# Attention scores and value products for two heads in turn, in the two halves of the array

## Chip, cores and metric

The kernel runs on one core of a Trainium2 chip. The metric is the device time of one execution in microseconds; lower is better. The core has a matrix engine (TensorE, in the profile PE for products and PEld for the loading of its stationary operand, called weights here), VectorE (DVE), ScalarE (ACT), GpSimd (POOL) and the transfer queues (SP among them). TensorE writes to eight banks of its accumulation memory, called P0 to P7 below.

## What is computed

One transformer layer in float32, for 256 tokens of 1024 features: an adaptive modulation, a token mixer (attention and retention beside each other, gated and projected), a norm, a gated feed-forward part with a short convolution, and another norm. The change concerns the attention alone. With 256 tokens there is one block, so the block selection of the reference falls away and what remains is causal softmax attention of 8 heads of 64 features:

```python
    def chunk(i):
        ...
        l_own = jnp.einsum('bhqd,bhkd->bhqk', qc, k_own).astype(jnp.float32) * scale
        l_own = jnp.where(causal, l_own, NEG_BIG)
        ...
        p = jax.nn.softmax(logits, axis=-1).astype(v.dtype)
        ...
        return (jnp.einsum('bhqk,bhkd->bhqd', p_own, v_own)
        ...
```

Queries and keys are rotated (rotary embedding) before; the outcome goes through `w_proj_moba`.

## The kernel before

**Main stream.** Nearly all time goes into products with weights that are read once. They arrive as units of 2048 columns (1 MB) in four `raw` buffers (`load_raw`, L71), and each unit is split into two halves of 1024 columns. A half is split into a high and a low part: ScalarE writes the high part (`whi`, L1001), VectorE the rest (`wlo`, L1015). `mm3` (L79 to L82) multiplies a tile by three matmuls: high by high, high by low, low by high. There are eight buffers for halves, and a planner (`prep_to`) keeps six halves split ahead of the products. The list `steps` holds one entry a half; the loop at the end of `_body` takes them in order. In attention's stretch a half is 12 matmuls of 512 columns, or 24 of 256. VectorE also reduces slices of `w_ada` (`ada`, L147) between the halves.

**Side streams.** Attention is a generator, `mixers()`, which the loop resumes three times a step: before the splits, after them, and after the products. Instructions are issued in the order of the program, each engine has its own queue in that order, and semaphores hold an instruction until its data are there. One turn `i` of the loop in `mixers()` (L801) is one step of the main stream. In it:

- before the splits, ScalarE scales the rows of head i-2 by one over their sum (L806) and takes exponentials of head i-1 (L810);
- after the splits, VectorE takes the reciprocal of the sums (L814); TensorE transposes the three 128 x 128 blocks of head i-TL (L819, TL = 4), and ScalarE copies them out (L821) to one of two buffers, 9a and 9b in turn;
- TensorE multiplies the values of head i-TL-1 by them (L831 with 256 moving columns, L832 with 128). The output has 64 rows; even heads take partitions 0 to 63 of P6, odd heads 64 to 127. After an odd head, `split` (L65, L66) brings the pair out as high and low parts;
- TensorE computes the scores of head i (L840, twice: 128 queries by 128 keys, and 128 by 256). The operands have 64 rows: partitions 0 to 63 of `qkT` hold an even head, 64 to 127 the odd one. Even heads write to P4, odd ones to P7. VectorE adds the mask and takes the maximum in one instruction for each of the two pieces (L847), and scales the maxima (L850);
- later parts of retention (`rope`, `rot_T` at L757) follow in some steps; then come the products of the step's half.

So scores run at i = 0 to 7, transposes at i = 4 to 11, and values at i = 5 to 12. Operands of attention are f32 and not split; the profile shows each such matmul as two loads of weights and two matmuls of the same line. Matmuls of the main stream are marked `fp32r` at their inputs and show one of each.

In the profile, `128*128`, `64*128` and `128*64` behind a matmul are the rows and columns of the array that it uses.

Of the kernel before, what the change touches and what calls it, by code (L numbers as in the profile page):

```python
# [13 lines left out]
HM, DM = 8, 64  # L14
# [36 lines left out]
def _body(nc, a, out, pe, act, dve, sp, cst, wts, big, tmp, ps, dram):  # L51
# [8 lines left out]
    def halves(n):  # L60
        """A [128, 8, 256] operand as two tiles of four k-tiles."""
        return [slot(n + e, [128, 4, 256], F32R) for e in "ab"]
# [21 lines left out]
    def table(func):  # L84
        """Brings the table of a function in ahead of its use."""
        d_ = tmp.tile([128, 1], F32, name="dummy", bufs=1)
        act.activation(d_, epst, func)

# [36 lines left out]
    # silu(c) along every partition  # L125
# [6 lines left out]
    def rows(dst, cols):  # L132
        """dst[every partition, 128 i + p] = cols[p, i]."""
        for c in range(2):
            p = bank(6 + c)
            for i in range(4):
                pe.transpose(p[:, i * 128:(i + 1) * 128],
                             cols[:, c * 4 + i:c * 4 + i + 1].to_broadcast([128, 128]), ident)
            act.activation(dst[:, c * 512:(c + 1) * 512], p, AF.Copy)
# [4 lines left out]
    def ada(raw, sec, j, rows=slice(0, 1024)):  # L144
        """Feature tile j of section sec of the modulation, its features on partitions."""
        junk = tmp.tile([128, 1024], mybir.dt.bfloat16, name="junk", bufs=1)
        dve.tensor_tensor_reduce(out=junk[:, rows], in0=raw[:, rows], in1=srow[:, rows], scale=1.0, scalar=0.0,  # L147
                                 op0=OP.mult, op1=OP.add, accum_out=mod[:, sec, j:j + 1])

# [6 lines left out]
    def h1(j, part):  # L156
        """Feature tile j of x (1 + scale) + shift."""
        if part == 0:
            ra = raws.pop(("ada1", j))
            if j == 0:  # L160
                ada(ra, 0, 0, slice(0, 512))
                dve.tensor_tensor(bcol[:, 0, 0:1], bcol[:, 0, 0:1], mod[:, 0, 0:1], OP.add)
            for i in range(2):
                ada(ra[:, i * 1024:(i + 1) * 1024], i, j, slice(512 if i == j == 0 else 0, 1024))
            dve.tensor_tensor(mod[:, 0:2, j], mod[:, 0:2, j], bcol[:, 0:2, j], OP.add)
            load_A()
        else:
            h32 = slot(("7a", "7b")[j % 2], [128, 256])
            act.activation(h32, raws.pop(("xT", j)), AF.Identity, scale=mod[:, 0, j:j + 1],
                           bias=mod[:, 1, j:j + 1])  # L170
            split(hh[:, j], hl[:, j], h32)
# [22 lines left out]
    def products_X(u):  # L194
        """The first gate's columns, of two feature tiles, in the banks that q and k leave for them. Two of
        them share a bank, so a product with zeros begins both."""
# [33 lines left out]
    main = []       # units: (source, None) or a slice of w_ada: (source, fn)  # L230
    steps = []      # (halves needed, halves done with, fn of their tiles)

    def weights(src, mm0, mm1):
        """A unit of two halves of 1024 columns; each is split, then used."""
        n = 2 * len(main)
        main.append(src)
        for i, mm in enumerate((mm0, mm1)):
            steps.append(((n + i,), (n + i,), lambda ts, mm=mm: mm(*ts[0])))

    def weights4(srcs, fns, needs):  # L240
        """Units whose halves are each used in several steps."""
# [132 lines left out]
    class Norm:  # L374
        """z = ALPHA x + g y piece by piece, its statistics and (z - mean) / std."""
# [22 lines left out]
        def more(self, c, w, p):  # L398
            """The rest of a sum of which add() had a part."""
# [15 lines left out]
        def shift(self):  # L415
            """-mean / std, for the scalar engine."""
            dve.tensor_scalar(self.sd[:, 2:3], self.mu, self.rstd, -1.0, op0=OP.mult, op1=OP.mult)
            self.nmr = self.sd[:, 2:3]
# [32 lines left out]
    def ln1_T(t):  # L451
        """Transposes of the normed tokens; scale and shift of the second modulation on the way out."""
# [9 lines left out]
    def ln1_hi(t, ks, whole=False):  # L462
        """On the scalar engine, the high parts, or the whole."""
# [14 lines left out]
    def ln1_half(t, c):  # L478
        """Four feature tiles; the two engines read different banks at a time."""
# [18 lines left out]
    def xs_group(src, xh, xl, t_bank, hooks):  # L498
        """Eight k-tiles x 512 columns, all of token tile 0 before token tile 1; with the high parts of a
        token tile before its low parts."""  # L500
# [45 lines left out]
    def out_tok1(q):  # L546
        """A quarter of the columns of token tile 1, so that little is left after the last product."""
# [19 lines left out]
    gh2, gl2 = (lambda k: S["h2h"][k // 4][:, k % 4]), (lambda k: S["h2l"][k // 4][:, k % 4])  # L567

    def up_tokens(t, p):
        """The first four tiles of the up projection come by tokens; turned here."""  # L570
# [61 lines left out]
    def out_rows(n, t, cs):  # L632
        """(z - mean) g / std + b, and the store; the first step of a piece comes before the second of the
        one before it, the first of all beside the square root."""
# [30 lines left out]
    def tok1(c, w):  # L665
        """The last quarter of the columns has a bank of its own for the last rounds, so that little is
        left after the last product."""
# [46 lines left out]
    later = []  # L714

    def ada_unit(secs, u, done):
        """Unit u (two feature tiles) of a section of w_ada; done() comes some steps after the last."""
# [7 lines left out]
    def rows_done(sec):  # L725
        """The section as a row on every partition, by way of DRAM: its features are eight to a partition."""
# [5 lines left out]
    def rope(x, cos, sin, pairs):  # L732
        """x = x * cos + (partner of x) * (signed sin) for heads of cos's length."""
# [19 lines left out]
    def rot_T(roped, t, dst, which, b):  # L753
        """Transposes of half a token tile's roped columns into dst[feature, group, token]."""
# [21 lines left out]
    def mixers():  # L776
        """Attention and retention beside the main stream. A step of the stream resumes this three
        times: before its splits, after them, and after its products."""
# [21 lines left out]
        blk = [slice(128 * qb, 128 + 256 * qb) for qb in range(2)]  # L800
        for i in range(HM + TL + 2):  # L801
# [11 lines left out]
            if 0 <= i - 1 < HM:  # L813
                dve.reciprocal(mx[:, 6:8], mx[:, 4:6])  # L814
            if 0 <= i - TL < HM:
# [7 lines left out]
            if 0 <= i - TL - 1 < HM:  # L823
                h = i - TL - 1
                pT = pt.pop(h)
                if h % 2 == 0:
                    S["pv"] = bank(6)
                p = S["pv"]
                s = slice(64 * (h % 2), 64 * (h % 2) + 64)
                c = slice(64 * h, 64 * h + 64)  # L830
                pe.matmul(p[s, 0:256], v[:, 0, c], pT[:, 0:256], start=True, stop=False)  # L831
                pe.matmul(p[s, 128:256], v[:, 1, c], pT[:, 256:384], start=False, stop=True)  # L832
                if h % 2:
                    split(yah[:, h // 2], yal[:, h // 2], p[:, 0:256])
            if i < HM:
                s = slice(64 * (i % 2), 64 * (i % 2) + 64)
                g = i // 2
                p = bank(4 + 3 * (i % 2))
                for qb, c in enumerate(blk):
                    pe.matmul(p[:, c], qkT[0][s, g, qb * 128:(qb + 1) * 128],  # L840
                              qkT[1][s, g, :128 + 128 * qb], start=True, stop=True)
                if i == 0:
                    sms = S["sms"] = slot(11, [128, TL + 2, 384])
                sm = sms[:, i % (TL + 2)]
                mx = tmp.tile([128, 8], F32, name="mx", bufs=TL + 2)
                for qb, c in enumerate(blk):
                    dve.tensor_tensor_reduce(out=sm[:, c], in0=p[:, c], in1=consts["mask"][:, 128 - 128 * qb:],  # L847
                                             scale=1.0, scalar=-3.0e38, op0=OP.add, op1=OP.max,
                                             accum_out=mx[:, qb:qb + 1])
                dve.tensor_scalar(mx[:, 2:4], mx[:, 0:2], -0.125, None, op0=OP.mult)  # L850
                st[i] = sm, mx
# [92 lines left out]
    def residual():  # L944
        """x1 = norm * g + b, and the rows of the second norm on all partitions."""
# [16 lines left out]
    # where the slices of w_ada for the later parts come in the stream  # L962
# [17 lines left out]
    def prep_halves():  # L980
        """Splits the halves in turn; the first part of one comes before the second of the one before it,
        where there is a buffer for it."""
# [177 lines left out]
```

## Time and profile before

| what | value |
|---|---|
| time, median of 3 runs | 445.71 us (445.6 to 446.73) |
| span of the profiled execution | 444.4 us |
| median less span | 1.3 us |
| TensorE busy | 427.8 us, 2732 matmuls |
| VectorE busy | 346.9 us |
| ScalarE busy | 242.2 us |
| attention's steps with scores or values | about 88 to 142 us |

The span is the time from the first to the last instruction of the execution that the profiler recorded; the time of a run holds some more on both sides. Busy time is the union of an engine's instructions. Matmuls overlap in the records, since one starts while the one before it still drains, so the distance from one start to the next says more than their length. The chain of waits gives that distance: every piece ends where the next one begins.

### The profile page before, as it was taken

How to read it: one execution, taken by the hardware profiler on the slowest of the kernel's cores; microseconds unless marked ns; L12 is line 12 of the kernel's file. 1: busy time of each engine (PE TensorE's matmuls, PEld its weight loads, DVE VectorE, ACT ScalarE, POOL GpSimd, SP SyncE). 2: the span in 40 equal slices, each digit the busy share in tenths (PEclk: the TensorE clock that was granted, in tenths of full speed). 3: DMA queues.
4: the chain of work that ended last, by engine and by line, in shares of the span. 5: the costliest groups of instructions: out<-in, count | busy, mean ns of one | idle time of the engine just before them, and what ended most of it. 6: DMA issues, size and time to landing. Idle time of an engine off the chain costs nothing.

```text
span 444.4 us, 6901 instructions
## 1 busy us (share of the span) xinstructions
PE 427.8 (96%) x2732; PEld 383.2 (86%) x2732; DVE 346.9 (78%) x547; ACT 242.2 (55%) x368; POOL 7.3 (2%) x17
## 2 busy tenths in 40 slices
PE   2999999999999999999999999999999999999993
PEld 1778888877777899999988899999999999999883
DVE  4888789976895989798788888698896765566476
ACT  4376578587774457643443896555454454455500
POOL 0000000000000000000000010000000000000000
PEclk9999999999999999999999999999999999999998
DMA  7999996886347678868745149577657764640001
GB/s 259 406 385 355 329 347 265 318 306 252 128 170 303 237 249 318 328 253 331 287 169 201 46 158 383 219 269 296 254 223 270 292 243 154 227 175 16 1 24 71
DMA packets 19728, 105.72 MB, mean 238 GB/s; under 512 B 2528, under 2 KB 4592, under 8 KB 8432
## 3 DMA queue, kind: packets, MB, share of 16 engines
q1 hardware_dynamic: 18288, 100.27, 60.2%
q0 software_dynamic: 1408, 5.01, 3.3%
q8 instruction: 21, 0.34, 0.3%
q14 instruction: 11, 0.09, 0.1%
HBM read 104.22 MB, written 1.06 MB: 237 GB/s over the span
## 4 chain that ended last, share of the span: by engine, by line
PE 92%; DVE 3%; DMA 2%; ACT 1%; SPq 1%; issue 0%; DVEq 0%
PE P L80 28%; PE P L82 27%; PE P L81 27%; DMA raw<-in_ada 2%; DVE junk L147 2%; PE P L840 2%; PE P L831 1%; PE P L757 1%; PE P L513 1%; PE P L515 1%; PE P L516 1%; SPq L73 1%; PE P L819 1%; DVE wlo L66 1%; ACT whi L65 0%; PE P L890 0%
## 5 line engine op out<-in xcount | busy, mean ns | idle before, releaser
L1015 DVE TENSOR_TENSOR wlo<-raw,whi 128x1024 fp32r<-128x1024 f32 x118 | 140.6, 1221 | 24.7 <-ACT whi L1001 24.7
L1001 ACT ACTIVATE whi<-raw 128x1024 fp32r<-128x1024 f32 x118 | 120.3, 1052 | 38.7 <-PE P L82 11.9
L82 PE MATMUL P<-whi,A 128*128 128x512 f32 (+1 forms) x228 | 87.2, 382 | 0.0
L80 PE MATMUL P<-whi,A 128*128 128x512 f32 (+1 forms) x184 | 73.0, 396 | 5.9 <-ACT A L65 5.7
L81 PE MATMUL P<-wlo,A 128*128 128x512 f32 (+1 forms) x184 | 70.8, 385 | 0.0
L147 DVE CUSTOM_DVE_ANT_0 junk<-raw,srow 128x1024 bf16<-128x1024 f32 (+1 forms) x49 | 58.8, 1200 | 1.5 <-DMA raw<-in_ada 1.1
L80 PE MATMUL P<-A3a,whi 128*128 128x256 f32 x192 | 54.4, 283 | 0.0
L80 PE MATMUL P<-A3b,whi 128*128 128x256 f32 x192 | 54.3, 283 | 0.0
L81 PE MATMUL P<-A6b,whi 128*128 128x256 f32 x192 | 54.3, 283 | 0.0
L82 PE MATMUL P<-A3b,wlo 128*128 128x256 f32 x192 | 54.3, 283 | 0.0
L82 PE MATMUL P<-A3a,wlo 128*128 128x256 f32 x192 | 54.3, 283 | 0.0
L81 PE MATMUL P<-A6a,whi 128*128 128x256 f32 x192 | 54.3, 283 | 0.0
L82 PEld LDWEIGHTS P<-whi,A 128*128 128x128 f32 x228 | 43.3, 190 | 8.8 <-DVE A L66 0.2
L80 PEld LDWEIGHTS P<-whi,A 128*128 128x128 f32 x184 | 35.1, 191 | 16.4 <-ACT A L65 7.6
L80 PE MATMUL P<-A,whi 128*128 128x256 f32 x160 | 45.9, 287 | 0.0
L82 PE MATMUL P<-A,wlo 128*128 128x256 f32 x160 | 45.2, 283 | 0.0
L81 PE MATMUL P<-A,whi 128*128 128x256 f32 x160 | 45.2, 283 | 0.0
L81 PEld LDWEIGHTS P<-wlo,A 128*128 128x128 f32 x184 | 35.1, 191 | 6.1
L81 PEld LDWEIGHTS P<-A6a,whi 128*128 128x128 f32 x192 | 36.8, 192 | 0.3
L80 PEld LDWEIGHTS P<-A3a,whi 128*128 128x128 f32 x192 | 36.8, 192 | 0.3
L80 PEld LDWEIGHTS P<-A3b,whi 128*128 128x128 f32 x192 | 36.9, 192 | 0.0
L81 PEld LDWEIGHTS P<-A6b,whi 128*128 128x128 f32 x192 | 36.9, 192 | 0.0
(231 smaller groups left out, 713.1 us busy)
## 6 DMA issues: line engine op xcount, KB each, us to landing
raw<-in_ada SPq DMA_DIRECT2D x23, 1024.0 KB, 6.2
raw<-in_wup SPq DMA_DIRECT2D x11, 1024.0 KB, 4.8
raw<-in_wgate SPq DMA_DIRECT2D x11, 1024.0 KB, 5.0
raw<-in_wdown SPq DMA_DIRECT2D x11, 1024.0 KB, 4.8
raw<-in_winB SPq DMA_DIRECT2D x10, 1024.0 KB, 5.8
raw<-in_winA SPq DMA_DIRECT2D x16, 256.0 KB, 7.0
raw<-in_winA SPq DMA_DIRECT2D x4, 1024.0 KB, 7.2
raw<-in_winGr SPq DMA_DIRECT2D x4, 1024.0 KB, 5.3
```

The source lines that it names most:

```text
L66: dve.tensor_tensor(lo, src, f(hi), OP.subtract)
L73: sp.dma_start(t[:, i * n:(i + 1) * n], src[:, i * n:(i + 1) * n])
L80: pe.matmul(o, lh, rh, start=start, stop=False)
L81: pe.matmul(o, lh, rl, start=False, stop=False)
L82: pe.matmul(o, ll, rh, start=False, stop=stop)
L147: dve.tensor_tensor_reduce(out=junk[:, rows], in0=raw[:, rows], in1=srow[:, rows], scale=1.0, scalar=0.0, op0=OP.mult, op1=OP.add, accum_o ...
L513: pe.matmul(p, xl(k)[:, tk], hi[:, c], start=False, stop=k == 7)
L515: pe.matmul(p, xh(k)[:, tk], hi[:, c], start=k == 0, stop=False)
L516: pe.matmul(p, xh(k)[:, tk], lo[:, c], start=False, stop=False)
L840: pe.matmul(p[:, c], qkT[0][s, g, qb * 128:(qb + 1) * 128], qkT[1][s, g, :128 + 128 * qb], start=True, stop=True)
L1001: act.activation(hi, src, AF.Copy)
L1015: dve.tensor_tensor(lo, src, f(hi), OP.subtract)
```

## The change

Scores are computed for a pair of heads in the steps with even i, up to 6; values for a pair at i = 6, 8, 10 and 12. Within a pair the matmuls of the two heads take turns: first piece of the even head, first piece of the odd head, second piece of each. The even head uses the lower half of the array's rows (scores) or columns (values), the odd head the upper half. Scores still go to P4 and P7, values to P6. The value products now stand ahead of the transposes of the same step, not behind them. VectorE's masking of both heads follows the scores of the pair. Transposes, exponentials and scaling stay one head a step.

The core of the diff (the rest takes out comments and docstrings):

```diff
+        def scores(h):
+            ps2 = [bank(4), bank(7)]
+            for qb, c in enumerate(blk):
+                for e in range(2):
+                    s = slice(64 * e, 64 * e + 64)
+                    pe.matmul(ps2[e][:, c], qkT[0][s, h // 2, qb * 128:(qb + 1) * 128],
+                              qkT[1][s, h // 2, :128 + 128 * qb], start=True, stop=True)
+            for e in range(2):
+                sm = S["sms"][:, (h + e) % (TL + 2)]
+                mx = tmp.tile([128, 8], F32, name="mx", bufs=TL + 2)
+                for qb, c in enumerate(blk):
+                    dve.tensor_tensor_reduce(out=sm[:, c], in0=ps2[e][:, c],
+                                             in1=consts["mask"][:, 128 - 128 * qb:],
+                                             scale=1.0, scalar=-3.0e38, op0=OP.add, op1=OP.max,
+                                             accum_out=mx[:, qb:qb + 1])
+                dve.tensor_scalar(mx[:, 2:4], mx[:, 0:2], -0.125, None, op0=OP.mult)
+                st[h + e] = sm, mx
+
+        def attend(h):
+            p = bank(6)
+            pT = [pt.pop(h + e) for e in range(2)]
+            for kb, (o, c) in enumerate(((slice(0, 256), slice(0, 256)), (slice(128, 256), slice(256, 384)))):
+                for e in range(2):
+                    pe.matmul(p[64 * e:64 * e + 64, o], v[:, kb, 64 * (h + e):64 * (h + e) + 64], pT[e][:, c],
+                              start=kb == 0, stop=kb == 1)
+            split(yah[:, h // 2], yal[:, h // 2], p[:, 0:256])
+
...
             if 0 <= i - 1 < HM:
                 dve.reciprocal(mx[:, 6:8], mx[:, 4:6])
+            if i % 2 == 0 and 0 <= i - TL - 2 < HM:
+                attend(i - TL - 2)
             if 0 <= i - TL < HM:
...
-            if 0 <= i - TL - 1 < HM:
-                h = i - TL - 1
-                pT = pt.pop(h)
-                if h % 2 == 0:
-                    S["pv"] = bank(6)
-                p = S["pv"]
-                s = slice(64 * (h % 2), 64 * (h % 2) + 64)
-                c = slice(64 * h, 64 * h + 64)
-                pe.matmul(p[s, 0:256], v[:, 0, c], pT[:, 0:256], start=True, stop=False)
-                pe.matmul(p[s, 128:256], v[:, 1, c], pT[:, 256:384], start=False, stop=True)
-                if h % 2:
-                    split(yah[:, h // 2], yal[:, h // 2], p[:, 0:256])
-            if i < HM:
...
+            if i < HM and i % 2 == 0:
                 if i == 0:
...
+                    S["sms"] = slot(11, [128, TL + 2, 384])
+                scores(i)
```

More of the change, by code (lines that the diff above doesn't have):

```diff
@@ L822, in mixers @@
                 pt[i - TL] = pT
-            if 0 <= i - TL - 1 < HM:
-                h = i - TL - 1
-                pT = pt.pop(h)
-                if h % 2 == 0:
-                    S["pv"] = bank(6)
-                p = S["pv"]
-                s = slice(64 * (h % 2), 64 * (h % 2) + 64)
-                c = slice(64 * h, 64 * h + 64)
-                pe.matmul(p[s, 0:256], v[:, 0, c], pT[:, 0:256], start=True, stop=False)
-                pe.matmul(p[s, 128:256], v[:, 1, c], pT[:, 256:384], start=False, stop=True)
-                if h % 2:
-                    split(yah[:, h // 2], yal[:, h // 2], p[:, 0:256])
-            if i < HM:
[L836 to L841, printed above, removed]
-                if i == 0:
[L843 to L851, printed above, removed]
+            if i < HM and i % 2 == 0:
+                if i == 0:
+                    S["sms"] = slot(11, [128, TL + 2, 384])
+                scores(i)
             if 0 <= i - RROPE < 4:
```

## The prediction

> **What bounds the kernel now.** I read the page first (part 1), then busy time by stage, then the waits of TensorE, to see whether TensorE is short of time or of work in the stage of the change.
>
> ```profile
> PE 427.8 (96%) x2732; PEld 383.2 (86%) x2732; DVE 346.9 (78%) x547; ACT 242.2 (55%) x368; POOL 7.3 (2%) x17
> ```
>
> ```profile
> 88.00:92.00 4.00, 4.00 (x18) 2.72 (x17) 2.65 (x8) 3.33 (x6) 0.00 (x0) 1.00 1.02 377
> ...
> 109.00:114.00 5.00, 5.00 (x25) 3.62 (x26) 4.07 (x11) 3.85 (x11) 0.00 (x0) 1.00 0.52 205
> 114.00:119.00 5.00, 5.00 (x25) 3.62 (x25) 4.49 (x12) 3.77 (x10) 0.00 (x0) 1.00 0.53 210
> 119.00:124.00 5.00, 5.00 (x25) 3.58 (x24) 4.25 (x11) 2.89 (x9) 0.00 (x0) 1.00 0.00 0
> 124.00:129.00 5.00, 5.00 (x29) 3.93 (x28) 4.93 (x10) 2.90 (x7) 0.00 (x0) 1.00 0.56 210
> 129.00:134.00 5.00, 5.00 (x29) 3.92 (x28) 4.59 (x9) 4.97 (x9) 0.00 (x0) 1.00 0.62 221
> ...
> 300.00:400.00 100.00, 100.00 (x728) 95.20 (x727) 72.09 (x97) 48.18 (x60) 1.08 (x2) 1.00 0.64 237
> ```
>
> ```profile
> PE P L80 <- ACT A L65: 5.7, 2, 5.4
> PE P L137 <- DVE sc L130: 3.1, 1, 3.1
> ```
>
> The columns of the windows are: length, then PE, weight loader, VectorE, ScalarE, GpSimd, then granted clock, share of DMA, GB/s. In each stage of attention TensorE is busy for the whole window at clock 1.00, and its only data waits, 8.8 us of two kinds, all lie in the first 60 us (asked for 60 us to the end, the view of waits has no row). So TensorE is the bound, and the question is what its busy time holds. The transfers are full at 88 to 92 us (1.02) and empty at 119 to 124 (0.00): by then they are ahead, and wait for buffers.
>
> A busy TensorE is not one that streams. The chain of waits gives each piece the time until the next one, and around the attention matmuls it is uneven:
>
> ```profile
> 81.23 0.88 PE P L757 x8
> ...
> 88.45 0.85 PE P L840 x4
> 89.30 0.43 PE P L80
> 89.73 0.23 PE P L81
> ...
> 107.78 0.33 PE P L819 x3
> 108.11 0.57 PE P L831 x2
> 108.90 0.85 PE P L840 x4
> 109.75 0.43 PE P L80
> 110.18 0.23 PE P L81
> ...
> 112.71 0.33 PE P L819 x3
> ...
> 122.89 0.57 PE P L831 x2
> 123.68 0.43 PE P L80
> ...
> 127.78 1.02 PE P L757 x8
> ...
> 142.00 0.63 PE P L890 x2
> ...
> 146.90 0.43 PE P L890 x2
> ```
>
> ```profile
> 107.39 0.48 PEld L819 LDWEIGHTS P<-first,A 128*128 128x128 f32 x3
> 108.04 0.19 PEld L831 LDWEIGHTS P<-A9a,A 128*64 128x64 f32 x2 [0.17 <-issue]
> 108.31 0.35 PEld L832 LDWEIGHTS P<-A9a,A 128*64 128x64 f32 x2
> 108.83 0.52 PEld L840 LDWEIGHTS P<-A3b,A3a 64*128 64x128 f32 x4 [0.17 <-issue]
> 109.68 0.19 PEld L80 LDWEIGHTS P<-whi,A 128*128 128x128 f32 x1 [0.33 <-issue]
> ```
>
> An f32 matmul appears as two passes (x2 for the one at L831, x4 for the two at L840). With 256 moving columns it takes 0.43 us in a steady run (146.90), with 128 columns 0.22 (L832: 108.90 - 108.11 - 0.57). I call the passes b = 0.215 and a = 0.11. One head's scores, or its values, are two passes of each: 0.65 us. The scores piece takes 0.85, so **0.20 us goes before its first pass**; the main product behind it takes 0.43 where 0.23 is usual, so **0.20 goes on the way out**. The values take 0.57 + 0.22 = 0.79: 0.14 on the way in. Out of them it is 0.20 before a matmul of the whole array (123.68, and 0.63 against 0.43 at L890), 0.14 before transposes (1.02 against 0.88). The loader's rows say why: at each change of the used part of the array (128 x 128, 128 x 64, 64 x 128) it is idle for "issue", though no data is missing, and the next weights are loaded after the array has emptied instead of beside the last pass. All this lies on the path.
>
> **Before, in sum.** Scores 8 x 0.85 = 6.80; out of scores 8 x 0.20 = 1.60; values 8 x 0.79 = 6.32; out of values in the five steps i = 8 to 12 that have no scores behind them 3 x 0.20 + 2 x 0.14 = 0.88. Together 15.60 us of TensorE.
>
> **The change part by part.** *Fewer changes of shape.* No matmul is added or dropped: 16 for scores and 16 for values remain. But scores come in 4 groups for 8 and values in 4 for 8. If a group's passes ran one after the other, as within one head today, a scores group would be 0.20 + 4a + 4b + 0.20 = 0.20 + 1.30 + 0.20 = 1.70, four of them 6.80. A values group is 0.14 + 1.30, four of them 5.76; out of it to the transposes three times 0.14 and once 0.20, 0.62. Together 13.18: **2.4 us saved without any overlap**, by rows of this trace, provided a change between the two halves costs nothing.
>
> *Overlap of the two halves.* No row shows two halves in flight at once, so this is bounded: nothing (13.18), or both heads wholly at once, 0.65 for a pair: 4 x 1.05 + 4 x 0.79 + 0.62 = 7.98, 7.6 us saved. Below nothing is the third rival. I take a value between, by the order of issue. The two passes of one matmul use the same half and stand next to each other, so the order is e0 e0 e1 e1 e0 e0 e1 e1. A pass starts no earlier than the one issued before it and not before its own half is free. For values (b b b b a a a a) the third pass then runs beside the second and the fifth and sixth beside the fourth; the last ends at 3b + 2a = 0.865. Loading does not disturb this: two loads of 64 columns start 0.055 apart (108.04: two of 0.134 in 0.19). For scores (a a a a b b b b) the passes alone would allow 2a + 3b = 0.865, but loads of 128 columns start 0.11 apart (four of 0.19 in 0.52), as long as an a pass. If the loader does one at a time, the first four passes cannot overlap, and only the seventh runs beside the sixth: 4a + 3b = 1.085. I take that, being the nearest row, and 0.865 as its other end (0.9 us over four groups).
>
> Scores 4 x (0.20 + 1.085 + 0.20) = 5.94; values 4 x (0.14 + 0.865) + 0.62 = 4.64; together 10.58. **Saved 15.60 - 10.58 = 5.0 us.** The profiled span is 444.4 us and the median of the runs 445.71, 1.3 us of it around the span; the difference carries over whole: 439.4 and **440.7**.
>
> The Trainium skill ("TensorE: Matmul & The Clock Gate", Part 3: Packing small matmuls) gives a packed group the length of one matmul plus about 4 ns for each further tile. By that the sum would be the upper end, 438.1 us. No row here shows it, and it is stated of neighbours that lie in different tiles, where here every second neighbour lies in the same one.
>
> *Order.* Values now stand ahead of the same step's transposes. They wait for ScalarE's copy of the step before, with that step's transposes, scores and all its main products queued behind on TensorE. The copy is early:
>
> ```profile
> 108.15 0.49 ACT L821 ACTIVATE A9b<-P 128x384 f32<-128x384 f32 x1 [1.12 <-PE P L819]
> ```
>
> It ends at 108.64, while the next step's attention begins with the transposes of 112.71, 4.1 us later; with steps shortened by a microsecond 3 us remain. Cost nothing; without that cover at most the copy's 0.49 in four steps, 2.0 us. The buffers turn over as before: the two score banks are written again two steps later, the transposed pair is read before its buffers are refilled.
>
> *VectorE.* The odd head's masking moves one step ahead:
>
> ```profile
> 104.87 0.29 DVE L847 CUSTOM_DVE_ANT_0 A<-P,mask 128x128 f32<-128x128 f32 x1 [0.94 <-PE P L840]
> ...
> 105.55 0.17 DVE L850 TENSOR_SCALAR mx<-mx 128x2 f32<-128x2 f32 x1
> ```
>
> That is 0.85 us a head, so even steps get 0.85 more and odd steps 0.85 less. From 109 to 134 us VectorE is busy for 22.3 of 25 us. There (i = 5 to 9) TensorE gives back 3 x (0.79 + 0.85 + 0.20) + 0.99 + 0.93 = 7.44, against 1.145 + 1.485 + 1.145 = 3.78, 3.7 us: the 25 become 21.3, and VectorE falls 1.0 us behind. What hides it is that weights are split six halves ahead, and that masks, exponentials, scaling and transposes of a head lie a step apart. Without that cover it costs 1.0 us.
>
> **Rivals.** *One kind of overlap fails* (13%). The halves of the values share all 128 rows, and two moving operands would have to enter the same rows. Values alone in series: 5.94 + 5.76 + 0.62 = 12.32, 3.3 us saved, 442.4. For it: nothing in this trace shows two inputs to the same rows. Against: nothing shows a limit. The skill's page (same section) says that weight loads overlap running matmuls only when their row groups differ, which is against an overlap of the values. The trace already departs from that: the second L831 load starts 0.055 us after the first, inside the first pass, with the same rows.
>
> *No overlap at all* (14%): 443.3, from fewer changes alone.
>
> *Full overlap* (7%): 438.1.
>
> *Slower: a change of half drains the array as a change of shape does* (9%). Each group has three changes between its halves, 24 in all. At the 0.20 and 0.14 of the rows, without overlap: 13.18 + 12 x 0.20 + 12 x 0.14 = 17.26, 1.7 us over before: 447.4. It decides from 2.42 / 24 = 0.10 us a change. For it: every change of the used part that the trace holds does drain. Against: each of these is a change of shape too, and none is a change of half alone. The skill ("TensorEngine Tiling (Array Packing)", Key Properties) says that a changed tiling mode drains TensorE and a changed tile does not; the first agrees with the 0.33 us of idle loader at 109.68, the second no run here shows.
>
> *The lead is lost to the supply* (10%). ScalarE, which splits the weights, waits for transfers in several places:
>
> ```profile
>   DMA raw<-in_winB: 6.3, 3
>   DMA raw<-in_wpr: 4.3, 2
> ```
>
> If the halves split ahead ran out there, a lead of 5.0 us would come back as a TensorE wait of up to 4.3: 445.0, no change. Against: TensorE waits for none of these today, six halves hold some 16 us of products (a half is 12 products of 0.23, 2.8 us), and the empty transfers at 119 to 124 us have 5 us to spare.
>
> **Numbers.** The forecast of 440.7 (439.8 with quicker loads) has 47%. About 0.3% (1.3 us) is what a measurement of this kernel tells from no change. Faster: 47 + 13 + 14 + 7 = 81%; same 10%; slower 9%. The range goes from the full overlap to no overlap with a little for scatter, 438.0 to 443.6, and leaves out the two last cases.
>
> **What would show it.** In the changed profile the chain should have four scores pieces of eight passes, near 0.20 + 1.085 = 1.29 us (1.07 with quick loads, 1.50 in series), and four values groups near 1.0 us (1.44 in series). The loader's idle "issue" rows should halve in number; such rows between two loads of one group would mean the fourth rival. TensorE should stay full from 60 to 400 us, with VectorE near 5 of 5 us around 110 to 130. The prediction is wrong if the groups shrink and the span does not, or if a group lasts over twice a single head's.

## The result and the profile after

| kernel | median | runs | ratio to before |
|---|---|---|---|
| before | 445.75 us | 445.6 to 446.73 | |
| changed | 439.13 us | 438.26 to 439.34 | 0.9846 (0.9832 to 0.986) |

The change makes the kernel faster by 6.6 us or 1.5%. Two later comparisons of the same kernel gave 0.983 (0.9808 to 0.9851) and 0.9838 (0.9821 to 0.9854), 7.1 us each. The forecast was 440.7, in a range of 438.0 to 443.6.

The first lines of the page after: the span falls by 7.0 us, and TensorE's busy time by 7.1 with the same number of matmuls.

```profile
span 437.4 us, 6902 instructions
PE 420.7 (96%) x2732; PEld 379.7 (87%) x2732; DVE 345.9 (79%) x547; ACT 241.4 (55%) x368; POOL 7.3 (2%) x17
```

The chain of waits after (start, length, piece); L809 is the scores, L828 the values, L852 the transposes, L898 the first matmul of retention:

```profile
89.15 0.86 PE P L809 x8
90.01 0.43 PE P L80
...
109.45 0.80 PE P L828 x8
110.25 0.48 PE P L852 x3
110.73 0.86 PE P L809 x8
111.58 0.43 PE P L80
...
134.29 0.80 PE P L828 x8
135.09 0.63 PE P L898 x2
```

A scores piece now holds eight passes, two heads, and lasts 0.86 us, where four passes of one head took 0.85. The values of a pair last 0.80, where those of one head took 0.57 + 0.22 = 0.79. The second head costs 0.01 us. From the first scores to the matmul behind the last values the stretch went from 142.00 - 88.45 = 53.55 us to 135.09 - 89.15 = 45.94: 7.6 us.

How that happens stands in the timeline of matmuls of one pair's values. The even head's operand is in buffer A9a, the odd head's in A9b:

```profile
109.38 0.43 PE L828 MATMUL P<-A9a,A 128*64 128x256 f32 x1
109.38 0.43 PE L828 MATMUL P<-A9b,A 128*64 128x256 f32 x1
109.64 0.38 PE L828 MATMUL P<-A9a,A 128*64 128x256 f32 x1
109.65 0.38 PE L828 MATMUL P<-A9b,A 128*64 128x256 f32 x1
```

Each pass of the odd head starts within 0.01 us of the same pass of the even head: not one pass later, as the prediction had it. The loader in the same stretch:

```profile
109.43 0.14 PEld L828 LDWEIGHTS P<-A9a,A 128*64 128x64 f32 x1
109.44 0.14 PEld L828 LDWEIGHTS P<-A9b,A 128*64 128x64 f32 x1
...
110.66 0.52 PEld L809 LDWEIGHTS P<-A3b,A3a 64*128 64x128 f32 x8 [0.17 <-issue]
111.51 0.19 PEld L80 LDWEIGHTS P<-whi,A 128*128 128x128 f32 x1 [0.33 <-issue]
```

Eight loads for the scores of two heads take the 0.52 us that four took for one. The idle loader before and after a group of scores (0.17, 0.33) is what it was; there are half as many groups.

TensorE's waits for data over the whole execution:

```profile
PE P L80 <- ACT A L65: 5.3, 1, 5.3
PE P L137 <- DVE sc L130: 3.1, 1, 3.1
PE P L757 <- ACT A3a L759: 0.7, 1, 0.7
```

The third is new. It lies at 85 us, ahead of attention, in a part that the change leaves alone, and it explains why the span lost 7.0 us where the stretch lost 7.6. In all eleven profiles of this document the part behind the stretch lasts 302.4 us, while the first scores start anywhere from 87.11 to 89.15 us. So the profiled executions differ in two places alone: in the stretch, which agrees to 0.02 us among the three of the changed kernel, and ahead of attention, where the code is the same in all. The length of the stretch is therefore the finer measure of what a change of attention is worth, and it is given below beside the medians.

### The profile page after: what moved, and what is told of

It is laid out like the page before. It is cut to its first block, busy times and chain, and to the rows that moved or that the text cites. A ratio compares the mean times of both kernels' runs of the same rounds, so it can differ in the third digit from the quotient of the medians.

```text
span 437.4 us, 6902 instructions
## 1 busy us (share of the span) xinstructions
PE 420.7 (96%) x2732; PEld 379.7 (87%) x2732; DVE 345.9 (79%) x547; ACT 241.4 (55%) x368; POOL 7.3 (2%) x17
## 4 chain that ended last, share of the span: by engine, by line
PE 83%; DVE 9%; ACT 3%; DMA 2%; issue 1%; SPq 1%; DVEq 0%; ACTq 0%
PE P L80 25%; PE P L82 25%; PE P L81 25%; DVE junk L147 3%; DMA raw<-in_ada 2%; DVE wlo L1023 2%; ACT whi L65 1%; DVE wlo L66 1%; PE P L513 1%; PE P L516 1%; PE P L515 1%; PE P L809 1%; PE P L828 1%; PE P L852 1%; SPq L73 1%
```

## The experiments

Theory F: two matmuls in different halves run wholly at once, and besides each group saves its changes of shape. Its rivals are the prediction's own partial overlap, and a gain from the fewer groups alone. The first four kernels ran on one chip beside 445.97 us for the kernel before.

**Scores alone.** The value products stand as before:

```diff
-            if i % 2 == 0 and 0 <= i - TL - 2 < HM:
-                attend(i - TL - 2)
...
+            if 0 <= i - TL - 1 < HM:
+                h = i - TL - 1
...
+                pe.matmul(p[s, 0:256], v[:, 0, c], pT[:, 0:256], start=True, stop=False)
+                pe.matmul(p[s, 128:256], v[:, 1, c], pT[:, 256:384], start=False, stop=True)
```

> Scores for pairs as in the change, values one head at a time as before. Theory F (the two halves run wholly at once: a pair's scores take 0.86 us in the chain, as the changed kernel's profile shows): scores 4 x 0.86 + 4 x 0.20 out, values 8 x 0.79 + 1.28 out, 11.84 us against 15.60 before: 3.8 us faster, near 442. Theory of the prediction (loader-bound, 1.285 us a group): 2.1 us faster. No overlap, fewer changes of shape only (1.50 us a group): 1.2 us faster.

Measured: 442.32 us, ratio 0.991 (0.9892 to 0.9928), 3.7 us faster. The scores pieces are 0.86, as F says, and the stretch is 138.27 - 88.53 = 49.74 us, 3.8 less than before.

**Values alone.** The scores stand as before:

```diff
-            if i < HM and i % 2 == 0:
-                scores(i)
+            if i < HM:
+                s = slice(64 * (i % 2), 64 * (i % 2) + 64)
...
```

> Values for pairs as in the change, scores one head at a time as before. Theory F (a pair's values take 0.80 us in the chain): scores 8 x 0.85 + 8 x 0.20 out, values 4 x 0.80 + 0.62 out, 12.22 us against 15.60: 3.4 us faster, near 442.4. Theory of the prediction (1.005 us a group): 2.6 us faster. Rival, the halves of the columns do not overlap (1.44 us): 0.8 us faster.

Measured: 442.38 us, ratio 0.9914 (0.9893 to 0.9935), 3.6 us faster, the values pieces 0.80. The stretch is 138.08 - 87.97 = 50.11 us, 3.4 less than before. The two parts add up to 7.3 us in the medians and 7.2 in the stretch, near the whole of 7.6: neither hides the other, and both kinds of halves overlap. The missing 0.4 fits the way out of the values, which the sum for the scores alone puts at 1.28 us and the sum before at 0.88.

**No overlap, same grouping.** The odd head's scores are computed from the even head's rows (its own are left out), so all eight passes of a group use one half:

```diff
-                    s = slice(64 * e, 64 * e + 64)
+                    s = slice(0, 64)
```

> The changed kernel, but the scores of the odd head are computed from the even head's queries and keys, in the same half of the rows (left out: the odd heads' scores). It takes the overlap of the scores away and leaves the fewer changes of shape. Theory F: a scores piece of 0.20 + 1.30 = 1.50 us against 0.86, 2.6 us slower than the changed kernel, near 441.7. Rival (the gain is the fewer changes of shape alone, and half the array or not does not matter): 0.86, near 439.1.

Measured: 441.42 us, ratio 0.9891 (0.9873 to 0.9909), 2.75 us over the head-by-head kernel below, on the same chip. Its chain:

```profile
88.35 1.50 PE P L809 x8
89.86 0.43 PE P L80
```

This is 0.20 + 1.30, the serial price of the prediction to the hundredth. Against 0.86 the overlap of the scores is worth 4 x 0.64 = 2.6 us, and the stretch, 136.85 - 88.35 = 48.50 us, is longer than the changed kernel's by just that. What the grouping alone gives to the scores is 8 x (0.85 + 0.20) - 4 x (1.50 + 0.20) = 1.6 us. So for the scores both causes are real, and the overlap is the larger. A pair's values in one half were not run: that they share out alike rests on the prediction's 1.44 us for such a group, which is an estimate.

**Does the order matter?** Both matmuls of the even head first, then both of the odd head:

```diff
-            for qb, c in enumerate(blk):
-                for e in range(2):
+            for e in range(2):
+                for qb, c in enumerate(blk):
...
-            for kb, (o, c) in enumerate(...):
-                for e in range(2):
+            for e in range(2):
+                for kb, (o, c) in enumerate(...):
```

> The changed kernel with both matmuls of the even head first, then both of the odd head; the groups and the changes of shape stay. Theory M (matmuls start in the order of issue, each as soon as its own half is free, both passes of it together): scores piece 0.20 + 2 x 0.215 + 0.44 = 1.07, values 0.14 + 3 x 0.215 + ... = 0.14 + 1.08 = 1.22 us, 2.6 us slower than the changed kernel, near 441.7. Rival P (the engine picks any matmul in its window whose half is free): pieces stay 0.86 and 0.80, no difference, 439.1. No overlap across heads: 1.50 and 1.44, 5.2 us slower, 444.3.

Measured: 438.67 us, ratio 0.9828 (0.9807 to 0.9849); it cannot be told from the changed kernel. The scores pieces are 0.86, the values 0.81, the stretch 133.85 - 87.87 = 45.98 us. Its timeline for one pair's values:

```profile
108.10 0.43 PE L828 MATMUL P<-A9a,A 128*64 128x256 f32 x1
108.11 0.43 PE L828 MATMUL P<-A9b,A 128*64 128x256 f32 x1
108.37 0.38 PE L828 MATMUL P<-A9a,A 128*64 128x256 f32 x1
108.38 0.38 PE L828 MATMUL P<-A9b,A 128*64 128x256 f32 x1
108.58 0.27 PE L828 MATMUL P<-A9a,A 128*64 128x128 f32 x1
108.60 0.27 PE L828 MATMUL P<-A9b,A 128*64 128x128 f32 x1
```

In the program the even head's 128-column matmul (108.58) stands ahead of the odd head's first (108.11), which starts 0.47 us before it. Theory M falls, and P holds for this order: TensorE starts a matmul whose half is free past one that waits for its own half. Taking turns in the program is not needed here; standing in one group is.

**How far ahead, and are larger groups better?** With the changed kernel once more on the same chip:

> The changed kernel once more, beside the other two on the same chip. 6.9 us faster than before, by the ratio measured first. The 0.7 us wait of the first transposes on ScalarE, seen in its first profile ahead of attention, should be absent if it is scatter of that execution, present if the change causes it.

Measured: 438.62 us against 445.73, ratio 0.983 (0.9808 to 0.9851). The wait of the first transposes is absent; it was scatter of one execution.

Four heads at a time: the scores of heads 0 to 3 in one group (two more banks, P5 and P6, are still free then), the values in two groups of four; the transposed operands of heads 2 to 5 go to their own scores' buffer.

```diff
+            ps2 = [bank(b) for b in (4, 7, 5, 6)[:n]]
...
+            if i in (TL + 4, TL + 8):
+                attend(i - TL - 4)
...
+            for g in range(2):
+                split(yah[:, h // 2 + g], yal[:, h // 2 + g], p[:, 256 * g:256 * g + 256])
...
+            if i in (0, 4, 6):
+                scores(i, 2 if i else 4)
```

> Scores of heads 0 to 3 in one group (step i = 0), 4 and 5 at i = 4, 6 and 7 at i = 6; values of four heads at a time at i = 8 and 12. Three scores groups for four and two values groups for four, the same passes. If a change of shape costs what the chain shows (0.20 and 0.14 in, 0.20 and 0.15 out), one scores group less saves 0.4 us and two values groups less 0.6: 1.0 us faster than the changed kernel, pieces of 0.20 + 1.30 = 1.50 for the four heads' scores and 1.44 for four heads' values. Rival: the four masks in one step (3.4 us of VectorE) hold back what follows, and the time is that of the changed kernel or more.

Measured: 438.13 us, ratio 0.9823 (0.9804 to 0.9842): by the medians not to be told from the changed kernel. In the profile the stretch, from the first scores (87.94) to the first matmul of retention (133.22 in the timeline of matmuls), is 45.28 us, about 0.65 less than after the change, where 1.0 was expected. The values of four heads are 1.45 us, as expected; a wait took most of the rest. ScalarE's timeline (start, length, instruction, idle time before it and what ended it):

```profile
116.60 0.39 ACT L65 ACTIVATE A<-P 128x256 fp32r<-128x256 f32 x1 [0.56 <-PE P L831]
119.15 0.39 ACT L65 ACTIVATE A<-P 128x256 fp32r<-128x256 f32 x1 [2.17 <-DVE A L66]
119.43 0.48 ACT L858 ACTIVATE A<-P 128x384 f32<-128x384 f32 x1
```

and TensorE's:

```profile
119.42 0.39 PE L82 MATMUL P<-whi,A 128*128 128x512 f32 x1
119.97 0.55 PE L856 MATMUL P<-first,A 128*128 128x128 f32 x3 [0.17 <-ACT A L858]
```

ScalarE starts the second `split` only when VectorE has done its half of the first one (L66), and VectorE has weights and a slice of `w_ada` in its queue ahead of that. The copy of the transposes (L858) stands behind it on ScalarE, and the next transposes of TensorE wait for that copy. They start 0.55 us after the matmul before them, where 0.23 is usual, so some 0.3 us is lost at their start. The expectation below, for a kernel with one split, puts the loss at 0.8 us; that figure adds the idle time of the loader (0.6) to that of TensorE (0.2) before the same three transposes.

The same with the first group in the order head 0, 2, 1, 3, to see how far ahead a free half is found:

```diff
-            for qb, c in enumerate(blk):
-                for e in range(n):
+            for e in (0, 2, 1, 3) if n == 4 else (0, 1):
+                for qb, c in enumerate(blk):
```

> As the kernel with four heads at a time, but the first group's scores stand in the order head 0, 2, 1, 3, both matmuls of each in a row, so that four matmuls (eight passes) of the lower half stand ahead of the first of the upper half. If the engine reaches that far ahead for a free half, the piece of 16 passes stays at 1.50 us. If it reaches one head ahead, as the order head by head has shown, and no further, head 1 starts only when head 2 has begun to load: 0.20 + 3 x 0.65 = 2.15, 0.65 us more. If heads in such an order do not overlap at all: 2.80.

Measured: 438.38 us, ratio 0.9825 (0.9808 to 0.9843). The loader with alternating heads:

```profile
87.94 1.18 PEld L809 LDWEIGHTS P<-A3b,A3a 64*128 64x128 f32 x16 [0.35 <-issue]
89.45 0.19 PEld L80 LDWEIGHTS P<-whi,A 128*128 128x128 f32 x1 [0.33 <-issue]
```

and with the two even heads first:

```profile
87.89 1.94 PEld L809 LDWEIGHTS P<-A3b,A3a 64*128 64x128 f32 x16 [0.35 <-issue]
90.16 0.19 PEld L80 LDWEIGHTS P<-whi,A 128*128 128x128 f32 x1 [0.33 <-issue]
```

From the first load to the next main product it is 1.51 us in turn and 2.27 with the even heads first. The middle case (2.15) is the nearest, and the single records of the trace bear it out: head 1's first pass starts at 88.66 us, with head 2's first (88.65) and behind the last of head 0 (88.44). The 0.1 us more than 2.15 lies in that first pass, which takes 0.21 us until the next one where a later pass takes 0.11. So TensorE found the other half past two matmuls of the busy one, as in the order head by head, and not past four; three was not run. The medians do not show these 0.76 us (438.38 against 438.13, with intervals that overlap), but the stretch does: 134.47 - 87.89 = 46.6 us against 45.28. The rest of that 1.3 us is mainly the wait of the transposes for ScalarE's copy, which is longer here: TensorE idles 0.65 us where it was 0.17.

**Four heads, one split.** One split of 512 columns for both pairs, to take the wait at 119.97 away:

```diff
-            for g in range(2):
-                split(yah[:, h // 2 + g], yal[:, h // 2 + g], p[:, 256 * g:256 * g + 256])
+            fl = lambda t: t[:, h // 2:h // 2 + 2].rearrange("p a b -> p (a b)")
+            split(fl(yah), fl(yal), p)
```

> The kernel with four heads at a time, with one split of 512 columns for the four heads' values in place of two of 256. In the first form ScalarE's second split waited 2.2 us for VectorE's half of the first, behind weights and a slice of w_ada in VectorE's queue, so that the copy of the transposes came late and TensorE stood for 0.8 us. If that wait took the gain, it is gone here: no wait of TensorE for the copy, and 1.0 us less than the changed kernel. If VectorE is simply full in this stretch, the wait comes back at another place and the time is that of the changed kernel.

> The changed kernel, beside the other one on the same chip: 7 us faster than before.

Measured: 437.17 us, ratio 0.9802 (0.9786 to 0.9818), against 438.65 for the changed kernel on the same chip, 0.9838 (0.9821 to 0.9854). It is the fastest of all, 1.5 us under the changed kernel by the medians. The chain has the larger pieces,

```profile
87.81 1.51 PE P L809 x16
89.32 0.43 PE P L80
...
114.90 1.45 PE P L831 x16
...
131.71 1.45 PE P L831 x16
133.16 0.63 PE P L902 x2
```

and the loader's waits in this stretch show what is left to lose:

```profile
PEld P L856 <- ACT A9a L858: 0.4, 1, 0.4
PEld P L910 <- ACT A3b L759: 0.2, 1, 0.2
PEld P L909 <- ACT A3a L759: 0.2, 1, 0.2
```

The stretch lasts 133.16 - 87.81 = 45.35 us, 0.6 less than after the change (45.94), and no less than with two splits (45.28). The wait at 119.97 is gone, but the expectation of no wait for a copy fails: a later group of transposes and the two retention matmuls behind it wait for ScalarE's copies at 127.5 us. In the chain these three pieces last 0.50, 0.64 and 0.28 us, where 0.33, 0.43 and 0.22 are usual, so they take 0.4 of the 1.0 us again. What the larger groups are worth is thus 0.6 us in both forms, and the one split is not shown to be better than two (0.9802 against 0.9823, with intervals that overlap). The spans of the two profiled executions, 435.5 us with one split and 436.4 for the changed kernel, differ by 0.6 in the stretch and by 0.3 ahead of attention (first scores at 87.81 against 88.07). The rest of the 1.5 us in the medians was not traced to a cause.

## Why the prediction was right, and where it was wrong

- **TensorE is the bound, and its time in attention goes to the end.** Right: 7.6 us less in the stretch, 6.6 to 7.1 us less in the kernel.
- **A change of shape costs 0.20 or 0.14 us in, and 0.20 or 0.14 out.** Right for the scores: the kernel in one half has 1.50 us and 0.43 behind it, the sum 0.20 + 1.30 and 0.20. For the values it agrees with the sum as a whole, but was not run by itself.
- **Overlap by order of issue: the step that failed.** "A pass starts no earlier than the one issued before it" and "if the loader does one at a time" gave 0.20 + 1.085 for a pair's scores and 0.14 + 0.865 for its values. Measured are 0.86 and 0.80, so 4 x 0.425 + 4 x 0.205 = 2.5 us more are saved: 5.0 + 2.5 = 7.5, near the 7.6 found. The rival of full overlap (7.6 us, 7%) was the true case. The range held because it reached from no overlap to full overlap, not because the term was right; the median of 439.13 lies nearer to the full overlap's 438.1 than to the forecast of 440.7. The four rows of loads 0.11 apart were read as the speed of the loader; they were the pace of one half, since eight loads in two halves take the same 0.52 us.
- **The Trainium skill's 4 ns for each further tile.** The prediction put it at the upper end of the saving, because every second neighbour lies in the same half. The trace agrees with the Trainium skill ("TensorE: Matmul & The Clock Gate", Part 3: Packing small matmuls): two heads take 0.01 us more than one. The Trainium skill says in the same section that loads overlap running matmuls only in other row groups; elsewhere in that section it allows a background weight buffer too. The limit to other row groups does not hold for the values here: 109.43 and 109.44 are loads of the two column halves, which share their rows, inside the passes begun at 109.38.
- **A change of half drains nothing.** Right: the loader has no idle "issue" inside a group, and the rival that was to be slower is out. The rival by which the values would not overlap is out too, by their 0.80 us.
- **Values ahead of the transposes cost nothing.** Right: TensorE has no wait at L828 or L852.
- **VectorE fills up, and its lead hides it.** Right, in the windows after (the third busy time is VectorE's):

```profile
105.00:110.00 5.00, 5.00 (x29) 3.77 (x28) 4.90 (x12) 4.24 (x13) 0.00 (x0) 1.00 0.87 326
110.00:115.00 5.00, 5.00 (x34) 3.73 (x30) 4.38 (x17) 4.33 (x14) 0.00 (x0) 1.00 0.93 344
115.00:120.00 5.00, 5.00 (x29) 3.72 (x28) 4.93 (x9) 4.45 (x11) 0.00 (x0) 1.00 0.00 0
120.00:125.00 5.00, 5.00 (x29) 4.26 (x28) 4.93 (x10) 3.02 (x7) 0.00 (x0) 1.00 0.60 210
125.00:130.00 5.00, 5.00 (x33) 3.89 (x32) 5.00 (x9) 4.97 (x9) 0.00 (x0) 1.00 0.59 213
```

TensorE is full in each of them, VectorE in nearly all. The transfers still run empty once (0.00 at 115), so the supply did not take the lead back.

## What to carry to other kernels

Small matmuls that use half the array cost two things that a busy TensorE hides: their own passes, and an emptied array on each side of the group, 0.14 to 0.20 us each here. Put them in groups with both halves filled. The order inside a pair did not matter: with two matmuls of the busy half ahead, the partner was found; with four, in a larger group, it was not. Larger groups than pairs gave 0.6 us of an expected 1.0 here: once TensorE is relieved, small waits for copies on other engines take back part of the next improvement, so look at what those engines' queues hold behind each evacuation. And where executions scatter by a microsecond or two, compare the length of the changed stretch in the profiles beside the medians.

## What was not expected of the hardware

- Two matmuls in different halves start within 0.01 us of each other, loads included, for halves of the rows and of the columns; 0.86 us for two heads' scores against 0.85 for one.
- TensorE starts matmuls out of the order of the program when their half is free: 0.47 us ahead of the one before it in the head-by-head kernel. With four matmuls of the busy half ahead it did not reach the fifth at once: 2.27 us against 1.51 for the group. Both hold for the two orders and the sizes run here.
